# The last layer's MLP as seven-product block products in two phases, activations through DRAM

## The chip, the core and the metric

The kernel runs on one core of one Trainium2 chip. The metric is device microseconds of one launch; three runs of the kernel before gave 2955.45 to 2957.43 us, median 2957.05 us.

## What is computed

The reference is a two-layer backbone on 1024 latent tokens and 256 context tokens of 1024 channels: layer 0 mixes tokens by a Fourier transform and a state-space scan, layer 1 by differential attention; each layer ends in an MLP with squared ReLU. Only layer 1's MLP is touched. With `h` the normed and modulated latent tokens (1024 x 1024) it is:

```python
def sq_relu_mlp(h, w1, w2):
    return jnp.square(jax.nn.relu(h @ w1)) @ w2      # w1 1024 x 4096, w2 4096 x 1024

x = x + g2 * sq_relu_mlp(modulate(rmsnorm(x, norm2_g[i]), sh2, sc2), mlp_w1[i], mlp_w2[i])
```

## The kernel before

Activations lie with channels on the 128 partitions and tokens along the free axis, so a tile of 128 channels by 512 tokens is the unit of most instructions. Every product is taken in three matmuls (`mm3`, L341 to L343): each operand is kept as a rounded high half and a remainder (`split`: a cast on ACT, L333, then a subtraction on POOL or VectorE, L337), and high*high, high*low and low*high are added up in PSUM. A matmul here is always a 128x128 weight tile against 512 tokens.

`second` runs layer 1. After the attention, `out_attn` projects and adds to `x` (tile `xL`, 8 rows of 128 x 1024), with `norm_hook` starting the norm of each token half as its last row is done; the norm's steps are handed out by `self.step()`. Then `mlp(1, ...)` starts: `up(f)` computes hidden block `f` (128 of 4096) for both token halves (`LAT`), each with 8 k-steps of `mm3` from `hb` (tokens 0 to 511) or `oS` (512 to 1023), then Relu and Square on ACT (L1465, L1466) and a split into one of three `H` buffers. `down` takes hidden blocks in pairs and adds their product to all 16 tiles of `x` by one VectorE instruction for each tile (L296, gate times PSUM plus `x`). The order is written out by hand: two ups, one down, and so on. Weight blocks come by the `Stream` `ws`: a 512 KB load on SP's queue into ring `R` (3 buffers), then a split into ring `W` (3 tiles), two blocks ahead. In the last down the hook `put` stores each finished 128x512 tile on SP's queue.

All engines take their instructions in program order. Ring `E` (5 tiles of 128x512) holds temporaries; a tile is taken again when its last reader is through.

## Time and profile before

| | us |
|---|---|
| median of three runs | 2957.05 |
| the profiled execution, its own time | 2952.55 |
| its span, first to last instruction | 2950.8 |
| layer 1's MLP in it, first matmul to the end of the span (2243.7 to 2950.8) | 707.1 |
| TensorE busy over the span | 2854.7 (97%) |

Times in the views are from the start of the span. PE is the matmul engine, PEld its weight loads, DVE VectorE, ACT ScalarE, POOL GpSimd, SP the engine that issues most DMAs. Matmuls overlap, so their pace is read from the distance of their starts or of what reads their results, not from the length of one.

### The profile page before, as it was taken

What the parts mean: (1) busy time and instruction counts of PE and PEld (TensorE: products, weight loads), DVE (VectorE), ACT (ScalarE), POOL (GpSimd) and SP (SyncE); (2) the same over time, 40 slices, a digit from 0 to 9 for tenths busy, and PEclk for the clock granted to TensorE, in tenths of its full rate; (3) what the DMA queues carried; (4) which work ended last, traced back from release to release, by engine and by line L of the source; (5) the groups of instructions that cost most, each with busy time, mean ns of one, the idle gap of its engine ahead of it and who ended that gap; (6) DMA issues with size and microseconds to landing.
All of it is one profiled execution on the core that took longest, in us unless ns stands there. A gap on an engine that the chain in (4) does not pass through costs nothing.

```text
span 2950.8 us, 39233 instructions
## 1 busy us (share of the span) xinstructions
PE 2854.7 (97%) x15186; PEld 2384.6 (81%) x15186; DVE 1732.3 (59%) x3533; ACT 1028.4 (35%) x1799; POOL 1149.0 (39%) x842
## 2 busy tenths in 40 slices
PE   5899999999999999999999999999999999999999
PEld 2666788788888888888778788999887888888887
DVE  7889868555543542323788838999966332232233
ACT  3341344222222122122434436666634223222221
POOL 5613223432232233233444426777715333333332
PEclk8898999999999999999999999999999999999999
DMA  7264630122222221111164633232232111111111
GB/s 291 89 187 159 197 111 24 65 79 72 77 89 78 72 89 56 34 43 43 49 201 125 156 113 118 71 97 79 69 107 65 51 43 53 47 43 58 50 44 71
DMA packets 179035, 263.30 MB, mean 89 GB/s; under 512 B 8736, under 2 KB 125984, under 8 KB 178336
## 3 DMA queue, kind: packets, MB, share of 16 engines
q1 hardware_dynamic: 168208, 233.53, 25.5%
q0 software_dynamic: 10640, 27.26, 3.1%
q8 instruction: 119, 1.95, 0.3%
q14 instruction: 68, 0.56, 0.1%
HBM read 210.92 MB, written 49.84 MB: 88 GB/s over the span
## 4 chain that ended last, share of the span: by engine, by line
PE 81%; DVE 9%; issue 3%; ACT 3%; POOL 2%; DMA 2%; SPq 0%; DVEq 0%; ACTq 0%; POOLq 0%
PE bank L341 22%; PE bank L342 21%; PE bank L343 21%; PE sc L1698 4%; PE pv L1738 4%; PE tb L1729 2%; DVE E L296 2%; DVE hl L296 1%; DVE S L296 1%; POOL E L324 1%; POOL E L427 1%; DVE S L1703 1%; DVE W L337 1%; PE bank L1573 1%; DMA hl<-in_ada_w_dram 1%
## 5 line engine op out<-in xcount | busy, mean ns | idle before, releaser
L296 DVE SCALAR_TENSOR_TENSOR xL<-bank,k,xL 128x512 f32<-128x512 f32 x544 | 404.1, 749 | 826.1 <-PE bank L343 825.7
L337 POOL TENSOR_TENSOR W<-R,W 128x1024 fp32r<-128x1024 f32 (+1 forms) x138 | 330.1, 2402 | 663.8 <-ACT W L333 373.1
L341 PE MATMUL bank<-H,W 128*128 128x512 f32 (+1 forms) x1280 | 474.0, 370 | 4.0 <-DVE xC L296 2.8
L342 PE MATMUL bank<-H,W 128*128 128x512 f32 (+1 forms) x1280 | 471.3, 368 | 0.0
L343 PE MATMUL bank<-H,W 128*128 128x512 f32 (+1 forms) x1280 | 471.2, 368 | 0.0
L333 ACT CAST W<-R 128x1024 fp32r<-128x1024 f32 (+2 forms) x180 | 178.2, 1009 | 672.0 <-PE bank L343 366.4
L337 POOL TENSOR_TENSOR H<-E,H 128x512 fp32r<-128x512 f32 (+1 forms) x160 | 191.2, 1195 | 441.4 <-ACT H L333 428.4
L341 PE MATMUL bank<-hl,W 128*128 128x512 f32 (+1 forms) x768 | 299.2, 390 | 8.0 <-ACT hl L433 3.7
L342 PE MATMUL bank<-hl,W 128*128 128x512 f32 (+1 forms) x768 | 296.0, 385 | 8.2 <-DVE hl L296 7.3
L343 PE MATMUL bank<-hl,W 128*128 128x512 f32 (+1 forms) x768 | 293.4, 382 | 1.1 <-DVE W L337 1.1
L341 PEld LDWEIGHTS bank<-H,W 128*128 128x128 f32 x1280 | 241.4, 189 | 45.7 <-DVE xC L296 3.9
L343 PEld LDWEIGHTS bank<-H,W 128*128 128x128 f32 x1280 | 241.5, 189 | 40.4
L342 PEld LDWEIGHTS bank<-H,W 128*128 128x128 f32 x1280 | 241.6, 189 | 39.8 <-issue 0.2
L1465 ACT ACTIVATE E<-bank 128x512 f32<-128x512 f32 (+1 forms) x160 | 88.8, 555 | 456.5 <-PE bank L343 456.5
L1703 DVE TENSOR_REDUCE S<-sc 128x1 f32<-128x1280 f32 x128 | 184.3, 1480 | 38.9 <-PE sc L1698 38.9
L341 PEld LDWEIGHTS bank<-hl,W 128*128 128x128 f32 x768 | 146.2, 190 | 58.6 <-issue 19.2
L342 PEld LDWEIGHTS bank<-hl,W 128*128 128x128 f32 x768 | 146.3, 190 | 40.2 <-DVE hl L296 12.9
L343 PEld LDWEIGHTS bank<-hl,W 128*128 128x128 f32 x768 | 146.1, 190 | 29.0 <-DVE W L337 1.5
L1698 PE MATMUL sc<-K,W 128*128 128x512 f32 x720 | 167.8, 369 | 0.0
L1738 PE MATMUL pv<-xL,wT 128*128 128x128 f32 x1280 | 155.8, 275 | 0.0
L324 POOL TENSOR_TENSOR R<-R,S 128x896 f32<-128x896 f32 x64 | 107.3, 1677 | 111.0 <-DVE S L296 87.6
L1738 PEld LDWEIGHTS pv<-xL,wT 128*128 128x128 f32 x1280 | 149.2, 192 | 0.1
(387 smaller groups left out, 5943.1 us busy)
## 6 DMA issues: line engine op xcount, KB each, us to landing
R<-in_w_dram SPq DMA_DIRECT2D x128, 512.0 KB, 3.6
R<-in_ada_w_dram SPq DMA_DIRECT2D x52, 512.0 KB, 3.7
W<-q_d POOLq DMA_DIRECT2D x15, 1024.0 KB, 5.4
A<-in_ada_w_dram SPq DMA_DIRECT2D x24, 512.0 KB, 4.4
hl<-in_ada_w_dram SPq DMA_DIRECT2D x20, 512.0 KB, 9.8
kk_d<-T SPq DMA_DIRECT2D x20, 512.0 KB, 3.2
...
R<-in_od_in_dram SPq DMA_DIRECT2D x18, 512.0 KB, 3.9
```

What stands on the lines that cost most here:

```text
L296: f(**kw)
L324: self.nc.gpsimd.tensor_tensor(out=o, in0=a, in1=b, op=op)
L333: nc.scalar.copy(hi, src)
L337: e.tensor_tensor(out=lo, in0=src, in1=hi.bitcast(F32), op=ALU.subtract)
L341: mm(ps, lhsT=lh, rhs=rh, start=first, stop=False)
L342: mm(ps, lhsT=lh, rhs=rl, start=False, stop=False)
L343: mm(ps, lhsT=ll, rhs=rh, start=False, stop=last)
L1465: self.nc.scalar.activation(out=e, in_=ps, func=AF.Relu)
L1698: nc.tensor.matmul(self.SC[i][:, c0:c0 + n], lhsT=Qf[:, e, q0:q0 + 128], rhs=K[:, i, c0:c0 + n], start=e == 0, stop=e == 1)
L1703: nc.vector.tensor_reduce(out=st[:, i, 1:2], in_=self.SC[i][:, 0:1280], axis=AX.X, op=ALU.max, negate=True)
L1729: nc.tensor.transpose(ps[:, 128 * j:128 * j + 128], it["P"][0][:, 128 * (c0 + j):128 * (c0 + j) + 128], self.ident)
L1738: nc.tensor.matmul(self.PV[:, 0:128], lhsT=it["wT"][:, kt], rhs=heads[h]["v"][:, kt], start=kt == 8, stop=kt == 3)
```

## The change

Layer 1's MLP goes through a new function `mlp_w`. Both matrix products are cut into 2 x 2 blocks and each block product is done with seven products in place of eight. The seven operands on the activation side are named `B11, B21, T2, T3, T1, B22, T4` (list `WINO`, in the order in which they are used); `T1` to `T4` are sums and differences of the quarters. On the weight side the seven are `A11, A12, S4, A22, S1, S2, S3`, also made from quarters.

The first phase computes the hidden activations. Hidden blocks 0 to 3 are still done plainly (`plain`); meanwhile `operands` forms `T1, T3, T2` of the normed tokens from their halves (`full` adds a tile's high and low half again) and `fourth` forms `T4`, in `B12`'s place, during the first unit. Units 2 to 15 follow, each four hidden blocks' quarters: 7 products of 12 matmuls (4 k-steps of `mm3`), each added from PSUM to one or two of four accumulators, then squared. `wino_weights` makes the weights: one load of 512 KB for each of two block pairs, four sums of 128x512 on VectorE, and seven splits (ACT and POOL); `make` keeps them five to six products ahead, two at a time. `results` turns a unit's four hidden tiles into the seven operands of the second phase one unit later, splits them into a staging row of `xL` and stores each (512 KB) to the DRAM tile `h_w`. `xL` itself is stored to `x_w` ahead of that.

The second phase (`c` 0 to 7, `q` 0 and 1) reads those operands back by `fetch`, a DMA on POOL's queue, one for each product into 24 slots (120 in all, with the eight of `x_w`), and does 7 x 2 products of 6 matmuls for each `c` and `q`, each added by VectorE to one of 28 accumulators. In the last `c`, `result` combines the accumulators (adds on POOL, `ptt`), applies gate and residual on VectorE and stores with `put`. The program counts 2712 matmuls of this MLP against 3072.

```diff
--- before.py
+++ after.py
...
+    WINO = ("B11", "B21", "T2", "T3", "T1", "B22", "T4")
+    def wino_weights(self, units):
+        raw = {}
+        def load(u, i):
+            if u < len(units):
+                raw[u, i] = self.R.v(1024)
+                for o, src in units[u][i][0](raw[u, i]):
+                    self.nc.sync.dma_start(out=o, in_=src)
+        load(0, 0)
+        load(0, 1)
+        yield
+        n, tile = 0, None
+        for u, pair in enumerate(units):
+            load(u + 1, 0)
+            A, S1, S2 = {}, None, None
+            for i, (_, names) in enumerate(pair):
+                for j, q in enumerate(names):
+                    A[q] = raw[u, i][:, 512 * j:512 * j + 512]
+            for i in range(7):
+                if i == 2:
+                    S1, S2 = self.E.v(512), self.E.v(512)
+                    self.tt(S1, A["21"], A["22"], ALU.add)
+                    self.tt(S2, S1, A["11"], ALU.subtract)
+                if i == 3:
+                    self.tt(A["21"], A["11"], A["21"], ALU.subtract)
+                if i == 5:
+                    self.tt(S2, A["12"], S2, ALU.subtract)
+                src = (A["11"], A["12"], S2, A["21"], S1, S2, A["22"])[i]
+                if n % 2 == 0:
+                    tile = self.W.next()
+                w = tile.v(2, 4, 128, o=1024 * (n % 2))
+                self.split(src, w[:, 0].rearrange("p a b -> p (a b)"), w[:, 1].rearrange("p a b -> p (a b)"), elo="p")
+                n += 1
+                if i == 5:
+                    load(u + 1, 1)
+                yield w
...
+    def mlp_w(self, layer, v0, oS, put):
+        nc, I = self.nc, self.I
+        v1, x8 = oS[:, :, :, 0:512], self.xL.v(8, SEQ)
+        t2, fb = self.buf("t2", 4096, True), self.buf("F", 2048)
+        dt = self.tc.dram_tile
+        xd, hd = dt([128, 8, SEQ], F32R, name="x_w"), dt([16, 7, 128, 1024], F32R, name="h_w")
+        for i in range(0, 8, 2):
+            nc.sync.dma_start(out=fl(xd)[:, i:i + 2], in_=x8[:, i:i + 2])
+        X, L = fb.v(4, 512), self.xL.v(4, 512)
+        turn = ([6, 7, 2, 3] * 27)[:105] + [6, 7, 6, 7, 6, 7, 6]
+        B = dict(B11=v0[:, :, 0:4], B21=v0[:, :, 4:8], B12=v1[:, :, 0:4], B22=v1[:, :, 4:8],
+                 T1=oS[:, :, 0:4, 512:1024], T3=oS[:, :, 4:8, 512:1024], T2=t2.v(2, 4, 512), T4=v1[:, :, 0:4])
...
+        units = [up_unit(u) for u in range(2, 16)] + [down_unit(c, q) for c in range(8) for q in range(2)]
+        gen, Wq, count = self.wino_weights(units), [], [0, -1]
+        def make(k=1):
+            for _ in range(k):
+                if count[0] < 7 * len(units) and 2 * (count[0] // 2 - 3) + 1 <= count[1]:
+                    Wq.append(next(gen))
+                    count[0] += 1
+        def results(u, C):
+            def keep(name, src, elo="p"):
+                o = x8[:, turn.pop(0)].rearrange("p (a b) -> p a b", a=2)
+                self.split(src, o[:, 0].bitcast(F32R), o[:, 1].bitcast(F32R), elo=elo)
+                nc.sync.dma_start(out=fl(hd)[u, self.WINO.index(name)], in_=o.rearrange("p a b -> p (a b)"))
...
+            keep("T1", T, "v")
...
+        def square(e, src):
+            nc.scalar.activation(out=e, in_=src, func=AF.Relu)
+            nc.scalar.activation(out=e, in_=e, func=AF.Square)
+        def operands():
+            for i in range(4):
+                x = {}
+                def full(q):
+                    x[q] = self.E.v(512)
+                    self.tt(x[q], fl(B[q][:, 0, i]), fl(B[q][:, 1, i]), ALU.add)
+                def keep(name, src):
+                    self.split(src, B[name][:, 0, i], B[name][:, 1, i], elo="p")
...
+        def fourth():
+            for i in range(4):
+                t, e = self.E.v(512), self.E.v(512)
+                self.tt(t, fl(B["T2"][:, 0, i]), fl(B["T2"][:, 1, i]), ALU.add)
+                self.tt(e, fl(B["B21"][:, 0, i]), fl(B["B21"][:, 1, i]), ALU.add)
+                yield
+                self.tt(t, e, t, ALU.subtract)
+                self.split(t, B["T4"][:, 0, i], B["T4"][:, 1, i], elo="p")
...
+        ops, late = operands(), fourth()
+        w = [self.ws.get(8, 128) for _ in range(3)]
+        for t0, n in LAT:
+            self.flush_norm(t0)
+            for f in range(3):
+                plain(f, w[f], t0, norms if t0 == 0 else lambda k: self.go(ops, 1))
+                if t0:
+                    self.ws.done()
+                    if f == 0:
+                        next(gen)
+        w, done = self.ws.get(8, 128), results(0, C[0])
+        plain(3, w, 0, lambda k: (make() if k % 2 else self.go(done, 1)))
+        plain(3, w, 512, lambda k: self.go(done, 1))
+        self.go(ops)
+        self.go(done)
+        self.ws.done()
+        make(6)
...
+        def fetch(n=1):
+            for _ in range(n):
+                i = len(tiles)
+                if i < len(order):
+                    o, tiles[o] = order[i], slots[i % len(slots)]
+                    src = xd[:, o[1]] if len(o) == 2 else hd[2 * o[0] + o[2], o[1]]
+                    nc.gpsimd.dma_start(out=tiles[o], in_=src.rearrange("p (a b) -> p a b", a=2))
+        bank = lambda: self.bank(0, 1, 2, 3, 4, 5, 6, 7)
+        done = results(1, C[1])
+        self.go(done, 2)
+        for u in range(2, 16):
+            a, b, c, d = ((X if u % 2 else L)[:, i] for i in (0, 1, 3, 2))
+            for j, name in enumerate(self.WINO):
+                ps, w, o = bank(), Wq.pop(0), B[name]
+                for k in range(4):
+                    self.mm3(ps, w[:, 0, k], w[:, 1, k], o[:, 0, k], o[:, 1, k], k == 0, k == 3)
+                count[1] += 1
+                if j == 0:
+                    nc.scalar.copy(a, ps)
+                else:
+                    for p, q in (((b, a),), ((a, a),), ((c, a),), ((a, a), (d, c)), ((a, a),), ((c, c),))[j - 1]:
+                        self.tt(p, ps, q, ALU.add)
+                if u == 2:
+                    self.go(late, 2)
+                make(2)
+                self.go(done, 1 + (u == 15))
+                e = {1: b, 4: d, 5: a, 6: c}.get(j)
+                if e is not None:
+                    square(e, e)
+                if u == 15 and j in (0, 1, 3):
+                    fetch(4 if j < 2 else 2)
+            self.go(done)
+            done = results(u, {"11": b, "12": a, "21": c, "22": d})
...
+        def result(q, e, j):
+            m, (dl, dh) = [M[q][2 * i + e] for i in range(7)], (2 * q + e, 4 + 2 * q + e)
+            def add(o, a, b, f=self.ptt):
+                f(m[o], m[a], m[b], ALU.add)
+            def end(i, d, t0):
+                x = fl(tiles["x", d])[:, t0 // 512]
+                self.stt(m[i], m[i], gate[:, d:d + 1], x, ALU.mult, ALU.add)
+                put(d, t0, m[i])
...
+            elif j == 4:
+                add(0, 0, 4)
+                add(4, 3, 4)
+                end(4, dh, 512)
...
+            elif j == 6:
+                add(6, 3, 6, self.tt)
+                end(6, dh, 0)
...
+                for j, name in enumerate(self.WINO):
+                    w = Wq.pop(0).rearrange("p h (f d) e -> p h f d e", f=2)
+                    for e in range(2):
+                        ps, m = bank(), M[q][2 * j + e]
+                        for p in range(2):
+                            b = tiles[c, j, p]
+                            self.mm3(ps, w[:, 0, p, e], w[:, 1, p, e], b[:, 0], b[:, 1], p == 0, p == 1)
+                        if c:
+                            self.tt(m, ps, m, ALU.add)
+                        else:
+                            self.vcopy(m, ps)
+                        if c == 7:
+                            result(q, e, j)
+                    count[1] += 1
+                    make(2)
+                    fetch(2 if c == 6 else 1)
+                    if c + q == 0:
+                        self.go(done, 1)
...
-        self.mlp_stream(1)
+        for f in range(4):
+            self.ws.add(self.I["w1"][1, f].rearrange("p a b -> p (a b)"))
...
-        H = [b(f"H{i}", 2 * SEQ, True) for i in range(3)]
...
-        self.mlp(1, LAT, LAT, H, put, before=lambda t0, n: self.flush_norm(t0))
+        self.mlp_w(1, v0, oS, put)
```

How the change moves instructions, at three places (`W` are weight splits, `xL<-` in POOL's rows operand splits of `results`, `H<-` the hidden activations of before).

POOL, inside the loop over hidden blocks, before: for four hidden blocks it splits four up weights and four down weights of 1024 columns and eight tiles of 512.

```order
L337 TENSOR_TENSOR W_190_21656<-R_243_21479,W_190_21656 128x1024
L337 TENSOR_TENSOR W_191_21661<-R_244_21542,W_191_21661 128x1024
L337 TENSOR_TENSOR H_72_18313<-E_605_21690,H_72_18313 128x512
L337 TENSOR_TENSOR H_72_18313<-E_606_21719,H_72_18313 128x512
L337 TENSOR_TENSOR W_192_21724<-R_245_21659,W_192_21724 128x1024
L337 TENSOR_TENSOR H_73_18317<-E_607_21753,H_73_18317 128x512
L337 TENSOR_TENSOR H_73_18317<-E_608_21782,H_73_18317 128x512
```

POOL, one unit of the first phase after:

```order
L337 TENSOR_TENSOR W_149_19026<-E_578_18979,W_149_19026 128x512
L337 TENSOR_TENSOR W_149_19026<-E_579_18980,W_149_19026 128x512
L337 TENSOR_TENSOR xL_2870<-F_18315,xL_2870 128x512
L337 TENSOR_TENSOR W_150_19069<-R_198_18898,W_150_19069 128x512
L337 TENSOR_TENSOR W_150_19069<-R_199_18938,W_150_19069 128x512
L337 TENSOR_TENSOR xL_2870<-F_18315,xL_2870 128x512
L337 TENSOR_TENSOR W_151_19112<-R_199_18938,W_151_19112 128x512
L337 TENSOR_TENSOR W_151_19112<-E_582_19116,W_151_19112 128x512
L337 TENSOR_TENSOR xL_2870<-E_580_19076,xL_2870 128x512
L337 TENSOR_TENSOR xL_2870<-F_18315,xL_2870 128x512
L337 TENSOR_TENSOR W_152_19159<-R_200_19032,W_152_19159 128x512
L337 TENSOR_TENSOR W_152_19159<-E_581_19115,W_152_19159 128x512
```

Five operand splits now stand among the seven weight splits of each unit.

DVE, behind the norm of the second token half (the rows into `oS`), before: the sums into `x` of the first down follow at once.

```order
L296 SCALAR_TENSOR_TENSOR E_550_18422<-xL_2870,k_106,Y_4_18373 128x512
L337 TENSOR_TENSOR oS_14120<-E_548_18412,oS_14120 128x512
L296 SCALAR_TENSOR_TENSOR oS_14120<-E_550_18422,k_102,oS_14120 128x512
L296 SCALAR_TENSOR_TENSOR E_552_18443<-xL_2870,k_106,Y_4_18373 128x512
L337 TENSOR_TENSOR oS_14120<-E_551_18429,oS_14120 128x512
L296 SCALAR_TENSOR_TENSOR oS_14120<-E_552_18443,k_102,oS_14120 128x512
```

DVE after, in the first unit of seven products (`t<-`: `T2` read for `T4`; the rows from `bank` are the sums of the second to fourth product):

```order
L296 TENSOR_TENSOR E_567_18726<-t_72_18311 128x512
L296 TENSOR_TENSOR E_568_18727<-hb_70_17910 128x512
L296 TENSOR_TENSOR E_567_18726<-E_568_18727,E_567_18726 128x512
L296 TENSOR_TENSOR xL_2870<-bank_1_18301,xL_2870 128x512
L296 TENSOR_TENSOR E_569_18749<-t_72_18311 128x512
L296 TENSOR_TENSOR E_570_18750<-hb_70_17910 128x512
L296 TENSOR_TENSOR E_569_18749<-E_570_18750,E_569_18749 128x512
L296 TENSOR_TENSOR E_566_18708<-xL_2870,F_18315 128x512
L296 TENSOR_TENSOR xL_2870<-bank_2_18302,xL_2870 128x512
L296 TENSOR_TENSOR E_571_18782<-t_72_18311 128x512
```

Three instructions with both inputs in SBUF now stand between two sums from PSUM, for each of four k-tiles.

DVE, the end of the program, before: one instruction for each tile of `x`, straight from PSUM.

```order
L296 SCALAR_TENSOR_TENSOR xL_2870<-bank_4_18306,k_102,xL_2870 128x512
L296 SCALAR_TENSOR_TENSOR xL_2870<-bank_5_18307,k_102,xL_2870 128x512
L296 SCALAR_TENSOR_TENSOR xL_2870<-bank_2_18304,k_102,xL_2870 128x512
L296 SCALAR_TENSOR_TENSOR xL_2870<-bank_3_18305,k_102,xL_2870 128x512
L296 SCALAR_TENSOR_TENSOR xL_2870<-bank_4_18306,k_102,xL_2870 128x512
```

DVE after, close to its end (`k_102` the gate, `oS` and `hb` the stored `x`; POOL's adds into `m` and `xL` run between them):

```order
L296 TENSOR_TENSOR m_21057<-bank_4_18304,m_21057 128x512
L296 SCALAR_TENSOR_TENSOR m_21057<-m_21057,k_102,oS_14120 128x512
L296 TENSOR_TENSOR m_21057<-bank_5_18305,m_21057 128x512
L296 SCALAR_TENSOR_TENSOR m_21057<-m_21057,k_102,oS_14120 128x512
L296 TENSOR_TENSOR xL_2870<-bank_6_18306,xL_2870 128x512
L296 SCALAR_TENSOR_TENSOR xL_2870<-xL_2870,k_102,hb_70_17910 128x512
L296 TENSOR_TENSOR xL_2870<-bank_7_18307,xL_2870 128x512
L296 SCALAR_TENSOR_TENSOR xL_2870<-xL_2870,k_102,hb_70_17910 128x512
L296 TENSOR_TENSOR xL_2870<-bank_0_18300,xL_2870 128x512
L296 TENSOR_TENSOR xL_2870<-m_21057,xL_2870 128x512
L296 SCALAR_TENSOR_TENSOR xL_2870<-xL_2870,k_102,oS_14120 128x512
```

Each gated sum stands directly behind the sum from PSUM, with POOL's add of the same tile due in between.

## Rows read from the trace of the kernel before

**Rows 1.** The page's first line: span and count of instructions.
```profile
span 2950.8 us, 39233 instructions
```
**Rows 2.** Busy us (count) by stretch: PE, PEld, DVE, ACT, POOL, then clock, DMA.
```profile
2500.00:2600.00 100.00, 100.00 (x443) 82.81 (x442) 30.17 (x41) 25.42 (x36) 32.91 (x18) 1.00 0.16 48
```
**Rows 3.** Timeline (start, length, idle before), end of the program, DVE and PE.
```profile
2945.31 0.75 DVE L296 SCALAR_TENSOR_TENSOR xL<-bank,k,xL 128x512 f32<-128x512 f32 x1 [0.61 <-PE bank L343]
2946.67 0.75 DVE L296 SCALAR_TENSOR_TENSOR xL<-bank,k,xL 128x512 f32<-128x512 f32 x1 [0.61 <-PE bank L343]
```
**Rows 4.** Timeline, start of the MLP: first matmuls of either half, norm's end.
```profile
2243.66 0.39 PE L341 MATMUL bank<-hb,W 128*128 128x512 f32 x1
2262.19 0.39 PE L341 MATMUL bank<-oS,W 128*128 128x512 f32 x1
2268.91 0.75 DVE L296 SCALAR_TENSOR_TENSOR oS<-E,k,oS 128x512 fp32r<-128x512 f32 x1
```
**Rows 5.** Groups by line and form, 2220 to 2950: count, busy, mean ns, idle before.
```profile
L337 POOL TENSOR_TENSOR W<-R,W 128x1024 fp32r<-128x1024 f32 x61 | 145.3, 2394 | 249.2 <-ACT W L333 249.2
L337 POOL TENSOR_TENSOR H<-E,H 128x512 fp32r<-128x512 f32 x64 | 83.2, 1301 | 211.2 <-ACT H L333 211.2
L296 DVE SCALAR_TENSOR_TENSOR xL<-bank,k,xL 128x512 f32<-128x512 f32 x256 | 192.2, 751 | 485.5 <-PE bank L343 485.5
```
**Rows 6.** Groups by line and form over the whole span.
```profile
L296 DVE TENSOR_TENSOR E<-bank,tab 128x512 f32<-128x512 f32 x68 | 44.0, 686 | 1.2
L337 DVE TENSOR_TENSOR hs<-E,hs 128x512 fp32r<-128x512 f32 x36 | 24.7, 687 | 1.6 <-ACT hs L333 1.6
L333 ACT CAST H<-E 128x512 fp32r<-128x512 f32 x128 | 79.6, 622 | 4.1
L1674 POOL DMA_DIRECT2D W<-q_d x15 | 12.1, 803 | 0.0
```
**Rows 7.** Timeline inside the norm, POOL.
```profile
2255.36 0.77 POOL L427 TENSOR_SCALAR E<-E,k,k 128x512 f32<-128x512 f32 x1
2256.09 1.31 POOL L324 TENSOR_TENSOR E<-xL,Y 128x512 f32<-128x512 f32 x1
2257.51 1.59 POOL L427 TENSOR_SCALAR E<-E,k,k 128x512 f32<-128x512 f32 x1
2259.07 1.74 POOL L324 TENSOR_TENSOR E<-xL,Y 128x512 f32<-128x512 f32 x1
...
2264.15 1.75 POOL L324 TENSOR_TENSOR E<-xL,Y 128x512 f32<-128x512 f32 x1
```
**Rows 8.** Timeline of the same stretch, DVE.
```profile
2257.87 0.75 DVE L296 SCALAR_TENSOR_TENSOR oS<-E,k,oS 128x512 fp32r<-128x512 f32 x1
2258.54 1.09 DVE L296 SCALAR_TENSOR_TENSOR E<-xL,k,Y 128x512 f32<-128x512 f32 x1
2259.79 1.57 DVE L337 TENSOR_TENSOR oS<-E,oS 128x512 fp32r<-128x512 f32 x1
...
2264.66 1.79 DVE L296 SCALAR_TENSOR_TENSOR oS<-E,k,oS 128x512 fp32r<-128x512 f32 x1
```
**Rows 9.** A long stretch with both engines full, 39.5 to 90.5: busy, then POOL and DVE groups.
```profile
39.50:90.50 51.00, 38.96 (x142) 24.45 (x142) 45.64 (x49) 16.02 (x26) 49.66 (x51) 0.79 0.43 153
...
L324 POOL TENSOR_TENSOR sw<-pw,cc 128x288 f32<-128x288 f32 x16 | 17.9, 1116 | 3.0 <-DMA cc<-in_ssm_ct_dram 3.0
L324 POOL TENSOR_TENSOR sw<-sw,tp 128x288 f32<-128x288 f32 x16 | 16.8, 1048 | 1.3
L324 POOL TENSOR_TENSOR tp<-pw,cc 128x288 f32<-128x288 f32 x16 | 16.1, 1007 | 0.0
...
L296 DVE SCALAR_TENSOR_TENSOR hl<-E,k,hl 128x512 fp32r<-128x512 f32 x13 | 15.6, 1200 | 0.0
L296 DVE SCALAR_TENSOR_TENSOR E<-xh,k,hl 128x512 f32<-128x512 f32 x13 | 15.3, 1184 | 2.8 <-ACT hl L409 2.8
L296 DVE TENSOR_TENSOR hl<-hl,E 128x512 f32<-128x512 f32 x7 | 7.7, 1098 | 0.4
```
**Rows 10.** DMA issues: count, KB each, median us from issue to landing.
```profile
kk_d<-T SPq DMA_DIRECT2D x20, 512.0 KB, 3.2
...
out_dram<-xL SPq DMA_DIRECT2D x16, 256.0 KB, 2.0
```

More of the change, by code (lines that the diff above doesn't have):

```diff
@@ L2045, in second, with put @@
         self.psum_std()
[L2046 removed]
         self.dump("x3", self.xL.v(8192))
[L2049 to L2053 removed]
+        def put(d, t0, src):
+            nc.sync.dma_start(out=self.out[:, d, t0:t0 + 512], in_=src)
+        self.mlp_w(1, v0, oS, put)
+        for h in (hb0, self.Y, oSb):
             h.free()
```

82 lines of the change are left out of this document (79 added, 3 removed).

## The prediction

> **What bounds the kernel now.** I read the span first (2950.8 us [rows 1]; the profiled execution took 2952.55 with what lies around it), then the busy time by stretch, then the starts of single instructions. Inside the MLP the matmul engine is busy 100.00 of 100 us at a granted clock of 1.00, while VectorE has 30, ACT 25 and POOL 33 [rows 2]. VectorE waits 0.61 us for a matmul ahead of each tile [rows 3]: nothing else is late. So here a matmul is worth its pace: six make one tile, tiles come 2946.67 - 2945.31 = 1.36 us apart [rows 3], which is 0.2267 us each. From the last tile's VectorE instruction to the span's end it is 2950.8 - 2946.7 = 4.1 us.
>
> **What is removed.** 3072 - 2712 = 360 matmuls, 360 x 0.2267 = 81.6 us, if the engine stays fed. A product of twelve takes 2.72 us, a unit of seven 19.04.
>
> **What is added: the prices.** A split's subtraction of 512 columns on POOL takes 1.30 us, of 1024 columns 2.39 [rows 5]; back to back I take 1.20 (half of 2.39), 1.25 as upper end. A VectorE add of 512 columns takes 0.69 us, from PSUM as from SBUF [rows 6]. An ACT cast takes 0.62 [rows 6]; a unit has 23 ACT instructions, about 14.7 of 19.04 us, so ACT is not the bound. A DMA issued on POOL takes 0.80 [rows 6].
>
> The decisive price is that POOL and those VectorE instructions that read both inputs from SBUF run one after the other. POOL's one-input instruction takes 0.77 us alone, its add 1.31 alone; beside VectorE the same forms take 1.59 and 1.74 [rows 7], and VectorE's take 0.75 undisturbed but up to 1.79 [rows 8]. The ends interlock: POOL ends at 2259.10, VectorE at 2259.63, POOL at 2260.81, VectorE at 2261.36 [rows 7, 8]. So a VectorE instruction holds POOL back for about 0.55 us, POOL's holds VectorE for about 1.18. The long stretch says that little is lost between: 48 POOL adds of 288 columns (1.18 x 288/512 = 0.66 us each, 32 us) and 33 large VectorE instructions (18 us) make 50 us, against 51 us of wall [rows 9]. VectorE's sums from PSUM do not take part: 256 of them average 0.751 while POOL works beside them [rows 5]. So I count P (POOL instructions, 1.20) and D (VectorE with two SBUF inputs, 0.55) as one queue.
>
> **The start.** The plain blocks take 16.3 us for 72 matmuls of the second half from 2262.2, then 48 more (10.9): to 2289.4 [rows 4]. Six products later, at 2305.7, unit 2 wants `T4`. The norm ends at 2269.7 [rows 4]; three activation splits that stood in it are gone, so the queue begins at about 2267. In front of the last `T4` tile stand, in program order: operands 24 D and 12 P, the plain blocks' `results` 6 D and 5 P, weights 4 D and 8 P, next `results` 4 D and 4 P, `T4` 12 D and 4 P. Together 50 D and 33 P: 27.5 + 39.6 = 67.1 us, so 2334. TensorE stands still for 28 us; with a few us for the chain VectorE, ACT, POOL of each tile I take **+30**, ends 28 and 40 (full lengths, 0.69 and 1.30).
>
> **The first phase and its hand-over.** A unit has 12 P (seven weights, five operands; two more go to VectorE) and 10 D (four weight sums, four differences, two splits): 14.4 + 5.5 = 19.9 us against TensorE's 19.04. Until the last weight made beside the first `results` of the second phase, the queue holds 175 P, 146 D and 17 DMA issues: 210 + 80.3 + 13.6 = 304 us. TensorE has 105 products there, 285.6. The difference, **+18**, is waited for by TensorE, in small pieces. Ends: +8 (P 1.17, the DMA issues beside D) and +27 (P 1.25). The new stores and loads, nine times 512 KB in a unit, are 4.7 MB in 19 us, some 248 GB/s; a store lands in 3.2 us [rows 10], and a staging row is wanted again four products (11 us) later, so I cost them at nothing. Where a store took over 8 us, ACT's next cast would wait and hold the squares and weight casts behind it.
>
> **The second phase.** A unit now has 7 P, 7 DMA issues and 4 D: 8.4 + 5.6 + 2.2 = 16.2 us, hidden beside 19.04. At `c` = 6 two issues for each product make 21.8, for two units: 5.5 us, covered by the five products in hand (13.6). The sums from PSUM are 14 x 0.65 = 9.1, hidden too.
>
> **The end.** In the last `c` VectorE and POOL take turns on one tile: sum from PSUM (0.65), POOL's add (1.25), gate (0.65), and VectorE stands behind POOL in order. By the rows of the order, the last half has: first product 1.3; second 2 x 2.55; third and fourth POOL's 4 x 1.25; fifth, two adds each, 2 x 3.8; sixth 2 x 2.55; seventh, on VectorE alone, 2 x 1.95. That is 28 us, where TensorE needs 19. The first half has the same, eight weight splits and four sums besides, half of them in gaps: 35. With the first product (2.7) and the last store (2.0 [rows 10]) the end takes 68 us from the first matmul of `c` = 7; before, the same place took 38.1 + 4.1. **+25**, ends 12 (the one queue alone, 49 us) and 32.
>
> **The sum.** -81.6 + 30 + 18 + 25 = -8.6 us. Ends: -81.6 + 28 + 8 + 12 = -34 and -81.6 + 40 + 27 + 32 = +17; a stall can bring the granted clock down (0.79 where TensorE was busy 39 of 51 us [rows 9]), which I cost at 0, with 5 more at the upper end. The profiled execution lies 4.5 us under the median of the runs, 2957.05; I take the change as a difference from the median: **2948.4 us**, 2923 to 2979 for this case.
>
> **Rivals.**
> *Both engines run side by side.* Then POOL alone paces the start (33 x 1.25 = 41 us from 2267: a stall of 3) and a unit's 15 us on POOL hide. -81.6 + 3 + 25: 2903. Against it: the interlocked ends [rows 7, 8] and the long stretch [rows 9].
> *VectorE waits out a whole POOL instruction each time*, slower than before. If whichever starts first keeps the other out to its end, each of the 10 D of a unit costs 1.20 + 0.55, and the seven sums from PSUM are not hidden: 10 x 1.75 + 7 x 0.61 = 21.8 us a unit. Over 13.4 units this is 37 us in place of 11.5, with the start at its upper end: -81.6 + 40 + 43 + 25 = +26, 2983. It ends slower from 20.5 us a unit on. For it: VectorE instructions of 1.57 and 1.79 us [rows 8]. Against it: a VectorE instruction that began at 2257.87 ran its 0.75 us straight through, though POOL's 1.59 us instruction had begun at 2257.51 [rows 7, 8], and the stretch of 51 us. The Trainium skill states this rule ("SBUF — State Buffer", Who interferes with whom): the pair of ports is an exclusive lock that the first to start holds for its whole instruction, for a VectorE instruction with two SBUF inputs against a GpSimd one that reads SBUF. The trace agrees that they exclude each other; the instruction at 2257.87 shows that the first to start does not always win.
> *POOL's DMA issues cost more in a row than the 15 of before.* At 1.6 us a unit of the second phase is 21.8 us on POOL: 15 x 2.8 = 42 more, 2990. Only single issues are in the trace [rows 6], so it stays open.
>
> **How the numbers follow.** A difference under 0.2% (5.9 us) can't be told from no change. Forecast 0.60: its range lies mostly under 2951.1, so 0.36 faster, 0.16 same, 0.08 slower. Side by side 0.13, all faster. VectorE waiting 0.19: 0.01, 0.04, 0.14. DMA issues 0.08, slower. Sums: faster 0.50, same 0.20, slower 0.30. The range 2921 to 2985 leaves out the first rival and the last, about 0.20.
>
> **What would show it.** Right: PE idle of about 30 us ahead of the product that reads `T4` with POOL busy through it; POOL near 100% through the first phase and units 19 to 20.5 us apart; the same POOL and VectorE forms as 1.2 to 1.9 us where they overlap; second-phase units at 19.04; 60 to 70 us from the first matmul of the last `c` to the end. Wrong: units at 19.04 with POOL idle (the engines don't exclude each other), units over 20.5, PE waiting for a DMA landing from `h_w`, or POOL's DMA issues well over 0.8 us.

## The result, and the profile after

The changed kernel takes 3003.4 us (median of 4 runs, 3002.49 to 3008.06), the kernel before beside it 2957.12: ratio 1.0161, 95% interval 1.0143 to 1.0178. It is 46 us slower, where 9 us faster was forecast. The profiled execution took 3002.49 us.

The page's first line, then the stretch of [rows 2] (columns as there):

```profile
span 3000.7 us, 39988 instructions
```
```profile
2500.00:2600.00 100.00, 92.66 (x391) 73.37 (x390) 74.32 (x78) 59.05 (x107) 86.86 (x57) 0.98 0.62 224
```

TensorE, full before, starts 391 matmuls there in place of 443, and no other engine is full either: POOL 86.86, VectorE 74.32 of 100 us. So the engines stand waiting for each other.

To see where the time went I cut every trace at four instructions: the first matmul of the plain blocks, ACT's copy after the first product of units 3 and 15, VectorE's first sum of `c` = 2 and of `c` = 7, and the span's end. Below, a column is one `c` of the second phase (two units, 168 matmuls, 38.08 us of TensorE). In the table, "TensorE" is the count of matmuls times 0.2267 us, and "forecast" the prediction's sum, cut at the same places.

| us | TensorE | forecast | changed kernel |
|---|---|---|---|
| start, to unit 3 | 65.3 | 97.5 | 107.2 |
| first phase, units 3 to 14 | 228.5 | (with the next) | 259.0 |
| hand-over, unit 15 to `c` = 2 | 93.9 | 340.4 | 111.6 |
| second phase, `c` = 2 to 6 | 190.4 | 190.4 | 202.8 |
| end, from `c` = 7 | - | 66.6 | 74.3 |

The forecast is passed by 9.7 us in the start, 30.2 in first phase and hand-over together, 12.4 in the second phase and 7.7 in the end: 60 us, all terms in one direction. (The medians miss the forecast by 55. Of the rest, 3.6 us are short gaps that the kernel before has too, and the two profiled executions lie differently far from their medians. One column of the second phase, `c` = 1, lies in the hand-over row: 3.0 of the 30.2.)

**First phase.** Units come 43.1 us for two, 21.6 each, where 19.9 was forecast. Groups over 2353 to 2590, eleven units (count, busy, mean ns, idle before it and what ended it), POOL, then VectorE:

```profile
L337 POOL TENSOR_TENSOR W<-E,W 128x512 fp32r<-128x512 f32 x35 | 55.2, 1583 | 19.6 <-issue 18.5 <-ACT W L333 1.1
L337 POOL TENSOR_TENSOR xL<-F,xL 128x512 fp32r<-128x512 f32 x20 | 33.0, 1651 | 9.1 <-issue 9.1
```
```profile
L296 DVE TENSOR_TENSOR xL<-xL,E 128x512 f32<-128x512 f32 x6 | 10.6, 1764 | 14.6 <-POOL xL L337 14.6
...
L296 DVE TENSOR_TENSOR F<-F,E 128x512 f32<-128x512 f32 x5 | 3.5, 692 | 21.7 <-POOL xL L337 21.7
```

POOL is idle 28.7 us, 2.6 a unit. VectorE waits 36.3 us for POOL, and at one instruction only: the last difference of `results`, `C["21"] - T`, which is written over `C["21"]`. One round of it in the timeline, VectorE, ACT, POOL:

```profile
2436.92 0.69 DVE L296 TENSOR_TENSOR F<-F,E 128x512 f32<-128x512 f32 x1 [4.34 <-POOL xL L337]
...
2438.91 0.68 DVE L296 TENSOR_TENSOR E<-R,E 128x512 f32<-128x512 f32 x1
```
```profile
2439.84 0.62 ACT L333 CAST W<-E 128x512 fp32r<-128x512 f32 x1
```
```profile
2435.58 1.31 POOL L337 TENSOR_TENSOR xL<-F,xL 128x512 fp32r<-128x512 f32 x1
2440.59 1.80 POOL L337 TENSOR_TENSOR W<-E,W 128x512 fp32r<-128x512 f32 x1 [3.70 <-issue]
```

POOL splits `B21` out of `C["21"]` (2435.58), last of all it has in hand. Only then may VectorE write that buffer (2436.92, after 4.34 us idle). Behind that in VectorE's order stands the next weight sum (2438.91), behind it ACT's cast (2439.84), behind it POOL's next split (2440.59): POOL has stood idle for 3.70 us.

**Start.** Waits of TensorE, 2240 to 2353 (us, times, longest):

```profile
PE bank L341 <- ACT xL L1624: 10.4, 3, 4.9
PE bank L341 <- ACT F L1624: 5.1, 1, 5.1
PE bank L341 <- ACT oS L333: 4.1, 2, 2.4
PE bank L342 <- POOL oS L337: 2.4, 2, 1.4
```

Most of it is not ahead of `T4` (the two rows with `oS`, 6.5 us) but in the plain blocks, where TensorE goes round two PSUM banks and waits 15.5 us for ACT to empty one. Which of them counts, the runs below say.

**Second phase.** Waits of TensorE, 2681 to 2886 (`c` = 1 to 5), and one in the timeline:

```profile
PE bank L341 <- DMA oS<-h_w: 7.3, 3, 2.5
PE bank L341 <- DMA hb<-h_w: 4.7, 4, 1.4
```
```profile
2777.16 0.39 PE L343 MATMUL bank<-hb,W 128*128 128x512 f32 x1
2778.73 0.50 PE L341 MATMUL bank<-hb,W 128*128 128x512 f32 x1 [1.18 <-DMA hb<-h_w]
```

Each column takes 41.06 us in place of 38.08, and TensorE waits for nothing but fetched tiles. By the program, the two tiles of the product `j` = 6 of `q` = 0 are issued after `j` = 2 and 3: two products, 5.4 us, between the last issue and its use. They land 5.1 to 5.3 us (median) after issue, and the issue itself stands on POOL behind two splits that wait for ACT.

**End.** Groups of VectorE, 2925 to the end:

```profile
L296 DVE SCALAR_TENSOR_TENSOR xL<-xL,k,hb 128x512 f32<-128x512 f32 x8 | 7.0, 878 | 18.5 <-POOL xL L324 18.5
...
L296 DVE SCALAR_TENSOR_TENSOR m<-m,k,oS 128x512 f32<-128x512 f32 x2 | 1.5, 752 | 8.0 <-POOL m L324 8.0
...
L296 DVE SCALAR_TENSOR_TENSOR m<-m,k,hb 128x512 f32<-128x512 f32 x2 | 1.5, 752 | 5.4 <-POOL m L324 5.4
```

VectorE stands idle for 31.9 of 75 us in front of twelve gates (gate times accumulator plus `x`), each behind an add on POOL.

### The profile page after: what moved, and what is told of

Read it like the earlier page. It is cut to its first block, busy times and chain, and to the rows that moved or that the text cites. A ratio compares the mean times of both kernels' runs of the same rounds, so it can differ in the third digit from the quotient of the medians.

```text
span 3000.7 us, 39988 instructions
## 1 busy us (share of the span) xinstructions
PE 2805.2 (93%) x14826; PEld 2323.7 (77%) x14826; DVE 2032.5 (68%) x3871; ACT 1123.5 (37%) x2027; POOL 1486.4 (50%) x1168
## 3 DMA queue, kind: packets, MB, share of 16 engines
q1 hardware_dynamic: 197712, 296.45, 30.5%
## 5 line engine op out<-in xcount | busy, mean ns | idle before, releaser
L337 POOL TENSOR_TENSOR W<-R,W 128x512 fp32r<-128x512 f32 (+1 forms) x198 | 360.3, 1829 | 443.5 <-issue 290.5
L296 DVE SCALAR_TENSOR_TENSOR xL<-bank,k,xL 128x512 f32<-128x512 f32 x288 | 211.9, 748 | 343.3 <-PE bank L343 342.9
L333 ACT CAST W<-R 128x512 fp32r<-128x512 f32 (+2 forms) x240 | 188.3, 804 | 524.4 <-PE bank L343 404.7
L341 PE MATMUL bank<-H,W 128*128 128x512 f32 (+1 forms) x768 | 274.8, 358 | 3.6 <-DVE xC L296 2.8
L342 PE MATMUL bank<-H,W 128*128 128x512 f32 (+1 forms) x768 | 272.0, 354 | 0.0
L343 PE MATMUL bank<-H,W 128*128 128x512 f32 (+1 forms) x768 | 272.0, 354 | 0.0
L341 PE MATMUL bank<-oS,W 128*128 128x512 f32 x568 | 229.8, 405 | 33.2 <-DMA oS<-h_w 13.2
L343 PE MATMUL bank<-oS,W 128*128 128x512 f32 x568 | 228.2, 402 | 13.2 <-POOL W L337 13.2
L342 PE MATMUL bank<-oS,W 128*128 128x512 f32 x568 | 226.7, 399 | 2.5 <-POOL oS L337 2.4
L337 POOL TENSOR_TENSOR H<-E,H 128x512 fp32r<-128x512 f32 (+1 forms) x96 | 108.3, 1129 | 229.9 <-ACT H L333 216.8
L337 POOL TENSOR_TENSOR W<-E,W 128x512 fp32r<-128x512 f32 x90 | 127.5, 1424 | 86.7 <-ACT W L333 64.3
L341 PEld LDWEIGHTS bank<-H,W 128*128 128x128 f32 x768 | 145.3, 189 | 25.2 <-DVE xC L296 3.9
L324 POOL TENSOR_TENSOR R<-R,S 128x896 f32<-128x896 f32 x64 | 107.3, 1677 | 111.2 <-DVE S L296 92.0
L343 PEld LDWEIGHTS bank<-H,W 128*128 128x128 f32 x768 | 145.3, 189 | 20.4
```

Of the source, the lines that this page charges most:

```text
L296: f(**kw)
L324: self.nc.gpsimd.tensor_tensor(out=o, in0=a, in1=b, op=op)
L333: nc.scalar.copy(hi, src)
L337: e.tensor_tensor(out=lo, in0=src, in1=hi.bitcast(F32), op=ALU.subtract)
L341: mm(ps, lhsT=lh, rhs=rh, start=first, stop=False)
L342: mm(ps, lhsT=lh, rhs=rl, start=False, stop=False)
```

## The experiments

Stage lengths as above, from each run's own trace; the last columns are the median and its ratio to the kernel before on the same chip (e14 and e15: one execution each).

| run | start | first phase | hand-over | second | end | us | ratio |
|---|---|---|---|---|---|---|---|
| changed kernel | 107.2 | 259.0 | 111.6 | 202.8 | 74.3 | 3003.4 | 1.0161 |
| e1_t_out | 104.1 | 239.4 | 114.5 | 205.4 | 75.7 | 2988.2 | 1.0118 |
| e2_lead | 107.3 | 259.1 | 112.1 | 207.1 | 73.9 | 3007.0 | 1.0182 |
| e3_dve | 113.2 | 299.4 | 116.2 | 189.0 | 62.8 | 3029.0 | 1.0257 |
| e4_end | 107.3 | 259.1 | 111.0 | 203.9 | 63.0 | 2993.5 | 1.0136 |
| e6_dve_late | 94.8 | 251.1 | 110.9 | 190.4 | 64.2 | 2955.6 | 1.0006 |
| e7_four | 104.0 | 239.5 | 114.5 | 190.4 | 63.0 | 2957.8 | 1.0009 |
| e8_banks | 107.3 | 259.1 | 112.5 | 202.1 | 74.3 | 3002.9 | 1.0162 |
| e9_mix | 104.2 | 268.6 | 114.4 | 188.0 | 64.1 | 2984.6 | 1.0100 |
| e10_late2 | 88.6 | 227.7 | 116.6 | 190.4 | 66.5 | 2938.5 | 0.9946 |
| e11_two_v | 107.2 | 238.5 | 113.2 | 190.4 | 62.5 | 2958.4 | 1.0018 |
| e12_no_early | 91.0 | 259.1 | 113.6 | 202.6 | 74.7 | 2988.6 | 1.0117 |
| e13_best | 88.6 | 228.3 | 115.3 | 190.4 | 63.4 | 2933.8 | 0.9930 |
| e14_no_store | 107.2 | 259.1 | 110.2 | 202.2 | 75.0 | 3001.7 | - |
| e15_best_no_store | 88.5 | 228.4 | 100.6 | 190.4 | 63.8 | 2919.5 | - |

### The ring of waits

```diff
-            self.tt(C["21"], C["21"], T, ALU.subtract)
-            keep("T4", C["21"], "v")
+            self.tt(T, C["21"], T, ALU.subtract)
+            keep("T4", T, "v")
```

> Edit: the last difference of a unit's results (C21 - T) is written over T and no longer over C21. Theory A (a circle of waits): in the changed kernel VectorE stands in order before this in-place difference until POOL has split B21 out of the same buffer, the next weight sums stand behind it, and then POOL itself is idle (28.7 us over 11 units, 2.6 a unit) because its next inputs come late. Without the wait a unit of the first phase goes from 21.58 us to 19.1-20.2, POOL's idle time nearly vanishes, and the time falls by 16 to 30 us: 2973 to 2987. Theory B (the queue of POOL and VectorE is itself full, each VectorE instruction standing behind a whole POOL instruction): the wait only moves elsewhere, units stay at 21.2 to 21.6, 2998 to 3004.

Measured: 239.4 us for twelve units, 19.95 each: theory A. The same work, one buffer changed. The hand-over and the second phase take 5.5 us back, so the total is 2988.2, 1.2 us over theory A's upper edge. The stretch 2400 to 2500 of the changed kernel, then of this one:

```profile
2400.00:2500.00 100.00, 93.62 (x394) 74.14 (x394) 76.65 (x80) 58.73 (x107) 88.94 (x57) 0.98 0.60 216
```
```profile
2400.00:2500.00 100.00, 98.32 (x428) 79.75 (x427) 86.72 (x83) 64.29 (x115) 97.32 (x61) 1.00 0.67 240
```

POOL goes from 88.94 to 97.32: now the queue of POOL and VectorE is full, and a unit takes about the 19.9 us that the prediction summed (the last ten units 20.05). That the queue alone sets the pace here is not shown by this: in e11_two_v below a sum of 18.6 gave the same pace.

### The fetch lead

```diff
-                if u == 15 and j in (0, 1, 3):
-                    fetch(4 if j < 2 else 2)
+                if u == 15 and j in (0, 1, 3, 4):
+                    fetch(4)
```

> Edit: sixteen activation tiles in place of ten are fetched during the last unit of the first phase, so each later fetch is issued six tiles earlier. Theory A (lead): a tile is issued as little as two products (5.4 us) before TensorE wants it and lands in 5.9 us; with the longer lead the columns c = 1 to 5 go from 41.06 us to 38.1-38.6 each, 12 to 15 us less, and the hand-over changes by no more than 5 us: 2984 to 2994. Theory B (rate): the transfers are short of bandwidth, as in the stretch with 382 GB/s, so the waits for landings return in the same amount at another place: 3000 to 3008.

Measured: `c` = 1 to 5 take 37.1 and four times 38.1 us, TensorE's own pace: lead, not rate. The total is worse, 3007.0, for a fault of the edit: with six tiles more in flight the double fetches at `c` = 6 reach a slot before its last use, `c` = 6 takes 54.8 us, and a tile is overwritten before it is used, so the last columns are computed from a wrong one. e7_four begins the double fetches later and has 38.1 in every column.

### POOL's work given to VectorE

The remainder of a split, written by its subtraction, is called its low half below.

```diff
-                self.split(src, w[:, 0].rearrange("p a b -> p (a b)"), w[:, 1].rearrange("p a b -> p (a b)"), elo="p")
+                self.split(src, w[:, 0].rearrange("p a b -> p (a b)"), w[:, 1].rearrange("p a b -> p (a b)"), elo="v")
...
-            def add(o, a, b, f=self.ptt):
+            def add(o, a, b, f=self.tt):
```

> Edit: all low-half subtractions of this MLP and the adds of the last c go from POOL to VectorE; POOL only issues transfers. Theory A (POOL and VectorE instructions with two SBUF inputs exclude each other, and POOL's takes 1.2 us where VectorE's takes 0.61): VectorE has 29 instructions of 0.61 us in a unit, 17.7 us, all of its forms take 0.6 to 0.7 us, units come at 19.0-19.8, the start stalls 10 to 15 us in place of 42 (83 x 0.61 = 51 us from 2267), the end takes 57 to 62 us in place of 75.6, the columns of the second phase stay at 41: 2915 to 2935. Theory B (the two engines work side by side and the loss is in waits between them): VectorE, nearly full and in order, delays the sums from PSUM, units stay over 21 us, 2985 to 3015.

Both theories fell: 24.95 us a unit is far from A, and B's premise is refuted by the prices. A weight sum of VectorE in the changed kernel (POOL busy beside it), then here (POOL empty), and this run's subtractions:

```profile
L296 DVE TENSOR_TENSOR E<-E,R 128x512 f32<-128x512 f32 x11 | 18.3, 1662 | 0.4
```
```profile
L337 DVE TENSOR_TENSOR W<-R,W 128x512 fp32r<-128x512 f32 x44 | 29.3, 687 | 9.9 <-ACT W L333 9.9
...
L337 DVE TENSOR_TENSOR W<-E,W 128x512 fp32r<-128x512 f32 x32 | 22.1, 691 | 17.8 <-ACT W L333 17.8
L337 DVE TENSOR_TENSOR xL<-F,xL 128x512 fp32r<-128x512 f32 x28 | 19.4, 691 | 19.0 <-ACT xL L333 19.0
...
L296 DVE TENSOR_TENSOR E<-E,R 128x512 f32<-128x512 f32 x11 | 7.6, 692 | 0.4
```

The price was right: 692 ns in place of 1662, so the two engines do exclude each other. The Trainium skill says so ("SBUF — State Buffer", Who interferes with whom); these two rows agree. Yet the unit got slower. VectorE waits for ACT's cast 102 times, 70.7 of 269 us in all: sum, cast, subtraction, with nothing between them in its order.

> Edit: as e3_dve (all low-half subtractions and the last adds on VectorE), but each subtraction is put one split later in VectorE's order, and the last difference of a unit's results is written over T. Theory A (e3_dve lost its time to the round trip VectorE difference, ACT cast, VectorE subtraction, 102 waits of 0.69 us in 269 us, while all forms took 0.68 us): with other work between, VectorE has its 29 instructions of 0.61 us, 17.7 us a unit; units 19.0 to 19.8 in place of 24.9, the columns of the second phase 38.1, the end 60 to 64: 2920 to 2945. Theory B (a VectorE this full and in order is late for the sums from PSUM anyway): units 21 to 22.5, 2955 to 2990.

The edit holds each subtraction back until the next split's cast has been put in line (`catch_up(1)` issues all held ones but the last):

```diff
+        self.nc.scalar.copy(hi, src)
...
+        def f():
+            self.nc.vector.tensor_tensor(out=lo, in0=src, in1=hi.bitcast(F32), op=ALU.subtract)
...
+        self.pend.append((key, f))
+        self.catch_up(1)
```

Measured 2955.6: 73 us less than e3_dve, by order (the last difference goes over T here too, which no run tried by itself beside an empty POOL). Units are 20.9 us, between the theories. The next run tests whether what is left stands at the units' ends, where the edit puts off nothing.

> Edit: as e6_dve_late (all low halves and last adds on VectorE), each subtraction now two splits later and without the flush between units, with the longer fetch lead and the eight banks of e7_four. Theory A (what e6_dve_late still lost, 20.95 us a unit at 18.0 us of VectorE, are the round trips to ACT that were left at the units' ends): units 19.0 to 19.8, columns 38.1, start 5 us better: 2920 to 2945. Theory B (the weights reach TensorE late because VectorE, at 86% and in order, is the bound in the unit's busy half): units 20.5 to 21, 2946 to 2960.

```diff
+        self.catch_up(1)
         self.nc.scalar.copy(hi, src)
...
-        self.catch_up(1)
...
             self.go(done)
-            self.catch_up()
```

The edit also issues the first load of the next unit's weights two splits later and drops the flushes ahead of loads and of the last weight sum, which the expectation does not name. With one split more between and no flush at the units' ends two units take 38.1 us, TensorE's pace, and the kernel 2938.5 us (ratio 0.993 to 0.9963). Its stretch 2400 to 2500:

```profile
2400.00:2500.00 100.00, 100.00 (x443) 82.80 (x442) 93.36 (x153) 66.49 (x118) 0.00 (x0) 1.00 0.70 248
```

Again 443 matmuls at 1.00, as [rows 2] before: VectorE alone, 93% busy, does what both engines together did not.

### Sharing between the two engines

Of e7_four's edits the eight banks are shown under "The start"; the later double fetch is this:

```diff
-                    fetch(2 if c == 6 else 1)
+                    fetch(2 if c == 6 and 7 * q + j > 5 else 1)
```

> Edit: four changes in four places, the low halves still on POOL: last difference over T (as e1_t_out), sixteen tiles fetched ahead with the double fetches begun later (as e2_lead, but no tile is overwritten before its last use), the last adds on VectorE (as e4_end), and the plain blocks' second half over eight PSUM banks in place of two. Theory A (the losses are in separate places and add up): units 20.05, columns 38.1, end 63, start as in e8_banks: 2948 to 2963. Theory B (what one place gains is lost at the next wait): 2970 or more.

2957.8, inside theory A's range: every place keeps its gain, but the hand-over takes 2.9 us back. It is the kernel before's time (ratio 0.9998 to 1.0021).

```diff
-                self.split(src, w[:, 0].rearrange("p a b -> p (a b)"), w[:, 1].rearrange("p a b -> p (a b)"), elo="p")
+                self.split(src, w[:, 0].rearrange("p a b -> p (a b)"), w[:, 1].rearrange("p a b -> p (a b)"), elo="v" if i < 2 else "p")
```

> Edit: as e7_four, with the low halves of the first two of seven weights on VectorE (their input comes from a load, not from a VectorE sum) and the other ten low halves on POOL. Theory A (the one queue: 10 x 1.2 + 12 x 0.55 = 18.6 us in place of 12 x 1.2 + 10 x 0.55 = 19.9, where e1_t_out measured 20.05 with POOL busy 97%): units 19.0 to 19.5, 7 to 12 us less than e7_four: 2945 to 2951. Theory B (as in e9_mix, a VectorE in order that waits for ACT and for POOL makes other weights late): units 20.5 to 21.5, 2962 to 2975.

Neither: 238.5 us for twelve units in place of 239.5, 2958.4. The stretch 2400 to 2500 of this run:

```profile
2400.00:2500.00 100.00, 98.25 (x427) 79.28 (x426) 83.59 (x95) 63.95 (x115) 77.13 (x50) 1.00 0.70 243
```

POOL falls from 97.32 in e7_four to 77.13 and the pace stays, so POOL's work is not what sets it here, and the sum of the queue (18.6 us) is not the pace. What is, I did not isolate; VectorE waits for ACT's casts again.

e9_mix is e7_four with e6_dve_late's held-back subtraction for the weights alone:

```diff
-                self.split(src, w[:, 0].rearrange("p a b -> p (a b)"), w[:, 1].rearrange("p a b -> p (a b)"), elo="p")
+                self.low(src, w[:, 0].rearrange("p a b -> p (a b)"), w[:, 1].rearrange("p a b -> p (a b)"), w)
```

> Edit: as e7_four, and the seven low halves of a unit's weights go from POOL to VectorE, each one split later in order; the results' five stay on POOL. Theory A (POOL and VectorE's two-input instructions are one queue, with POOL's 1.2 us and VectorE's 0.61): 5 x 1.2 + 17 x 0.61 = 16.4 us a unit, under TensorE's 19.04; units 19.0 to 19.8, columns 38.1, end 60 to 63: 2925 to 2943. Theory B (a VectorE instruction waits out a whole POOL instruction each time it meets one, and in order holds the sums back): units 20.5 or more, 2955 or more.

Theory B by its sign: 22.4 us a unit. Of this run, 2400 to 2560, VectorE's largest group and TensorE's main wait:

```profile
L1571 DVE TENSOR_TENSOR W<-R,W 128x512 fp32r<-128x512 f32 x29 | 28.6, 996 | 1.4 <-ACT W L1568 1.4
```
```profile
PE bank L343 <- DVE W L1571: 17.2, 14, 2.3
```

A subtraction takes 996 ns, not 687, though POOL is busy only 30%: five splits on POOL are enough to stretch VectorE and to make weights late. In e6_dve_late, with the same hold and POOL empty, a unit takes 20.9 us, and the same wait in the same stretch is short:

```profile
PE bank L343 <- DVE W L1571: 1.7, 7, 0.4
```

Seven low halves moved cost 29 us of first phase, all twelve and in good order win 12. The sum of the queue (16.4 us here) does not give the pace.

### The start

```diff
-            ps, (hh, hl) = self.bank(0, 1), self.hv(t0, 512)
+            ps, (hh, hl) = self.bank(*((0, 1) if beside is norms else range(8))), self.hv(t0, 512)
```

> Edit: the plain blocks' second half and the fourth block go round eight PSUM banks in place of two. Theory A (in the start TensorE waits 15.5 us for ACT to empty one of two banks, ACT standing in order before casts whose inputs are late): TensorE runs ahead, the start loses 10 to 16 us less, 2987 to 2994. Theory B (the queue of POOL and VectorE ahead of T4 sets the start, and TensorE only comes earlier to the same wait): 0 to 4 us, 2998 to 3004.

Theory B: 107.3 in place of 107.2. The 15.5 us of waits for evictions, the largest in the list above, cost nothing: TensorE waits elsewhere and comes to the last tile of `T4` at the same time, 94.9 us after its first matmul in the changed kernel and 95.0 here:

```profile
2340.69 0.80 PE L341 MATMUL bank<-oS,W 128*128 128x512 f32 x1 [2.38 <-ACT oS L333]
```
```profile
2339.80 0.80 PE L341 MATMUL bank<-oS,W 128*128 128x512 f32 x1 [2.38 <-ACT oS L333]
```

```diff
-                self.split(src, o[:, 0].bitcast(F32R), o[:, 1].bitcast(F32R), elo=elo)
+                if u > 1:
+                    self.split(src, o[:, 0].bitcast(F32R), o[:, 1].bitcast(F32R), elo=elo)
```

> Edit: the splits of the results of units 0 and 1 (the plain blocks) are left out, ACT casts, ten low halves on POOL and four on VectorE; what is stored for these two units is what the rows held, so the output is not the reference's. All else as in the changed kernel. Theory A (the queue of POOL and VectorE ahead of T4 sets the start): 10 x 1.2 + 4 x 0.55 = 14 us leave it, the start (first matmul of the plain blocks to the first product of unit 3, 107.2 us) gets 12 to 16 us shorter, the rest stays: 2987 to 2992. Theory B (ACT, in order before its casts, or the chain of sum, cast and subtraction for each T4 tile sets it): 0 to 6 us shorter, 2997 to 3004.

Theory A: the start takes 91.0 us, 16.2 less, for 14 us of queue. So the work that stands in order ahead of `T4` sets the start. The edit does not tell the engines apart, for fourteen casts on ACT go with the low halves; and the sum on POOL and VectorE alone is not enough, for e3_dve, with POOL empty, took 113.2 us, and e6_dve_late, with little but the order changed, 94.8.

### The end

The edit is the second hunk of e3_dve's, alone.

> Edit: only the adds of the last c go from POOL to VectorE. Theory A (VectorE and POOL take turns on one tile and VectorE stands idle behind POOL in order): the end from the first matmul of c = 7 goes from 75.6 us to 57-63: 2984 to 2992. Theory B (the end is set by the weight splits, or by the chain of adds whichever engine makes them): less than 5 us gained, 2998 to 3004.

Theory A: 63.0 in place of 74.3 us. The median of the two runs came out 1.5 us over its range: in the profiled one (2995.8) the MLP began 4 us later (its first matmul 2249.7, in the changed kernel 2245.8), and the other (2991.3) is inside.

In e10_late2 TensorE waits in the end only for weights, 2871 to 2939:

```profile
PE bank L343 <- DVE W L1567: 19.0, 3, 10.3
```

```diff
                     make(2)
+                    if c == 7:
+                        self.catch_up()
```

> Edit: e10_late2 with two differences: the fetch lead of the changed kernel again (ten tiles), and in the last c no subtraction is held back past its own product. Theory A: in the end of e10_late2 TensorE waits 19.0 us for subtractions of weights that were held until just before their product, behind the adds of the result; without the hold the end goes from 66.5 us to 50-56. And since POOL issues the fetches with nothing in front of them, the short lead is enough (columns stay at 38.1, as in e6_dve_late) and the burst at the hand-over is smaller (110.9 us there from unit 15 to c = 2, against 116.6): 2917 to 2928. Theory B (the last adds on VectorE bound the end whatever the weights do; the hand-over is bound by all its transfers): 2934 to 2940.

Theory B in both parts: the end takes 63.4 (VectorE busy 19.36 of 20 us from 2870, 57.2 of the last 64: now mostly its own work), and the hand-over 115.3. All the same 2933.8, the fastest that leaves nothing out: ratio 0.993, interval 0.9918 to 0.9942.

### The hand-over

```diff
-                nc.sync.dma_start(out=fl(hd)[u, self.WINO.index(name)], in_=o.rearrange("p a b -> p (a b)"))
+                for s in {4: (4, 14), 6: (6, 15), 14: (), 15: ()}.get(u, (u,)):
+                    nc.sync.dma_start(out=fl(hd)[s, self.WINO.index(name)], in_=o.rearrange("p a b -> p (a b)"))
```

> Edit: as the changed kernel, but the fourteen stores of the results of units 14 and 15, 7.3 MB that fall in the hand-over, are left out; what stands at these places is written earlier, beside units 5 and 7 (copies of the results of units 4 and 6), so the output is not the reference's. Theory A (the hand-over is short of transfers: 382 GB/s there, ACT waits 12.3 us for stores, TensorE 10 us for fetched tiles): from unit 15's first product to c = 1 it takes 58 to 64 us in place of 70.5, the rest stays: 2989 to 2997. Theory B (the hand-over is lost on VectorE and POOL, as the units before it: VectorE waits 16.3 us there for POOL's splits): 68 us or more, 2999 to 3005.

Theory B: 69.2 to `c` = 1 in place of 70.5 (110.2 to `c` = 2 in place of 111.6), though the transfers fell from 387 to 173 GB/s in 2630 to 2650. VectorE waits in 2590 to 2680, here:

```profile
DVE xL L296 <- POOL xL L337: 10.3, 1, 10.3
DVE F L296 <- POOL xL L337: 6.6, 2, 4.3
```

The largest is the ring again, with the same 10.3 us in the changed kernel: there the split of `B21` stands on POOL behind two runs of four fetch issues, 2.90 and 2.87 us. But without the ring (e1_t_out) the hand-over is not shorter: 114.5 us, and ACT waits 21.4 us for stores there (2575 to 2690).

> Edit: e13_best with the stores of units 14 and 15 left out as in e14_no_store (output not the reference's). Theory A (once the queue of POOL and VectorE is out of the way, the hand-over is bound by transfers: 386 to 393 GB/s for 60 us in e13_best, ACT waits 37 us for stores and VectorE 20.7 us behind ACT): from unit 15's first product to c = 2 it takes 97 to 106 us in place of 115.3, 2918 to 2927. Theory B (as in e14_no_store, another wait stands in the same place): 111 us or more, 2929 to 2935.

Here theory A: 100.6 in place of 115.3. With the ring and POOL's splits gone, the transfers bound the hand-over; whether by their rate, or because a staging row is free only when its store has landed (8.1 us, median of 2560 to 2660 in e13_best, 3.0 in 2400 to 2500), the edit does not tell. The stretch 2560 to 2640 of e13_best, then of this run (last: clock, DMA share, GB/s):

```profile
2560.00:2640.00 80.00, 65.76 (x257) 51.41 (x256) 55.31 (x91) 26.58 (x47) 24.90 (x35) 0.89 1.17 379
```
```profile
2560.00:2640.00 80.00, 75.08 (x322) 60.76 (x321) 69.19 (x114) 30.66 (x54) 26.18 (x37) 0.98 1.09 326
```

## Why the prediction was wrong

**What is removed** held: where TensorE is fed, a column takes 38.08 us and two units 38.1, 0.2267 us a matmul.

**The prices** held as far as they can be seen alone: the engines exclude each other (692 against 1662 ns), and sums from PSUM take no part (0.68 us beside a busy POOL). With the ring taken out a unit takes 19.95 us for 19.9; but e11_two_v took 19.9 for a sum of 18.6, and e9_mix 22.4 for 16.4. No unit came out below its sum, and these came out above. The step that failed is the reading of that sum as a pace: it took one queue for one that is always full. POOL and VectorE each work in order and wait for each other's results, and the prediction looked only at how much each had to do, never at what an instruction overwrites. It counted the in-place difference among four as 0.55 us of work, and neither its wait nor what stood behind it; that alone is 19.6 us (e1_t_out).

**The rival that came out nearly right was wrong too.** "VectorE waits out a whole POOL instruction" gave 21.8 us a unit and 2983; units took 21.6. But e1_t_out touched no price and no lock, and had 19.95. A forecast's number is no proof of its mechanism. One of the prediction's arguments against it was weak all the same: VectorE's instruction at 2257.87 need not have overtaken one of POOL's that was at work. VectorE's instruction before it, also with two inputs in SBUF, ran until 2257.95, and POOL's, begun at 2257.51, may have been waiting for its end:

```profile
2256.82 1.13 DVE L337 TENSOR_TENSOR oS<-E,oS 128x512 fp32r<-128x512 f32 x1 [2.73 <-ACT oS L333]
```

**The start**, +30 with ends 28 and 40, took 107.2 - 67.5 = 39.7 (67.5 is TensorE's 65.3 and the 2.2 us that the kernel before loses there). Right in kind, work ahead of `T4` (e12, e8), with the value at the upper end; the sum of the two engines' work as its measure is not shown, as e3_dve's start was longer with less of it. Part of the value is the restart: in the waits for `T4`, four of 1.07 to 2.38 us between 2333 and 2343, the granted clock fell from 1.00 to 0.5, the lower of its two levels (1.2 of 2.4 GHz), and behind the last tile TensorE runs on at 0.52:

```profile
2343.00:2348.00 5.00, 5.00 (x13) 3.86 (x13) 1.08 (x2) 1.04 (x2) 3.20 (x3) 0.52 0.20 79
```

13 matmuls in 5 us where 22 fit, 2 us. The "PE idle of about 30 us ahead of the product that reads `T4`" was not to be seen: the stall is spread over the plain blocks, and the wait that counts is the shorter one.

**The hand-over** lies in the same term as the first phase, +18 with ends 8 and 27; the two measured 30.5 and 14.7. The first phase's part was mis-sized by the ring (e1). In the hand-over of the changed kernel, leaving the stores out gave 1.4 us (e14) and taking out the ring alone gave nothing (e1: 2.9 us longer): which wait sets it there stays open. The transfers, costed at nothing, bound it once the ring and POOL's splits are gone (e15), with the sign that the prediction had named, a store of over 8 us that holds ACT's cast: 8.1 us in e13_best.

**The second phase** was costed at nothing: "7 P, 7 DMA issues and 4 D", 16.2 us, hidden. POOL was not full there, and the columns `c` = 1 to 5 still lost 3.0 us each and `c` = 6 0.6, 15.4 in all. The prediction asked how long POOL was busy and not when each tile had been asked for. Its own list named the sign, TensorE waiting for a landing from `h_w`. Two independent cures show the two halves of the cause: a longer lead (e2, e7), or a POOL with nothing in front of the issues (e3, e6, e13, with the short lead): 38.1 a column either way.

**POOL's DMA issues** took 0.73 us each (78 in 56.4 us); that rival is out.

**The end**, +25 with ends 12 and 32, is 7.7 more: 32.7. The turns between VectorE and POOL were the right mechanism (e4: 11.3 us less) and their sum was too short in both halves: the first took 38.3 us for 35, the second 32.8 for 28. In each, one gate stood behind weight splits on POOL besides the add (6.94 and 4.00 us), where the prediction put half of the splits into gaps and none into the second half.

**The range**, 2921 to 2985, ended 18 us short: its upper ends were added up from sums of work, and two of the losses, the ring and the fetch lead, are no work.
